# One load of a gate's attention outputs per head pair, sample transfers regrouped, and another emission order in a hybrid attention layer

## The chip, the cores and the metric

The kernel runs on one core of a Trainium2 chip. A core has four compute engines with queues of their own: TensorE (PE, matmuls and transposes into PSUM), VectorE (DVE), ScalarE (ACT) and GpSimd (POOL). A fifth queue, SyncE (SP), issues the transfers (DMA). Engines wait for each other through semaphores, and each queue runs in the order in which the program wrote it. The metric is the device time of one execution in microseconds, the median of several runs.

## The reference

One layer works on a prompt of 1024 tokens and on a sample of 32 tokens that has a cache of 512 past positions. The width is 1024, with 8 heads of 64 in group A (chunked band attention with a relative-position bias) and 8 in group B (stick-breaking attention). All is float32.

```python
hn = rmsnorm(h, g_pre)
qa, ka, va, ga, qb, kb, vb, gb = split(hn @ w_in)        # 1024 x 4096
oa = band_attention(qa, ka, va)       # softmax over the own 64-frame chunk and 8 before it
ob = stick_breaking(qb, kb, vb)       # w = sigmoid(z) * prod(sigmoid(-z)) over later keys
y  = concat(oa * silu(ga), ob * silu(gb)) @ w_out
h  = h + rmsnorm(y, g_post)
h  = h + sigmoid(h @ w_ple_gate) * (p @ w_ple)
```

The outputs are `h` of prompt and sample, and the new keys and values of both groups, for prompt and sample apart.

## The kernel before, in words

Every float32 product is made of three passes: an operand is split into a high part and the rest, and high x high, high x low and low x high are summed in PSUM. The names `wh`/`wl`, `hnh`/`hnl`, `wTh`/`wTl` and `kd`/`kl` are such pairs.

**Stages.** The first stage normalises nine row tiles of 128 (the ninth holds the 32 sample tokens), turns them into `hnh`/`hnl`, and makes the first columns of the input projection. Then come eight stages, one for each pair of heads (A0, B0, A1, B1, ... A3, B3). While stage n computes the attention of its pair (two heads), the projections q, k and v of the next pair (`col_steps`, matmuls named `mm_`, in three chunks of 352 tokens) fill TensorE. In stage 7 there is no next pair, and the eight gate projections (`mm_gA`, `mm_gB`) fill it. Two of the A stages and two of the B stages also carry the attention of the sample (`sample_attention`, four heads at a time). The last stage makes the second input (`ple`), the output projection (group products named `o0P` to `o3P`, seven products by a Strassen-like scheme for each half) and the gate projection (`g0P` to `g3P`), with normalisation and the final sum.

**Attention of a tile.** `scores` multiplies 128 queries with their keys into one or two PSUM banks of tag S (three buffers). Group B takes two sigmoids of each piece on ScalarE, a multiplying scan from the last key back on VectorE, and a product on GpSimd. Group A adds the bias on VectorE and takes an exponential on ScalarE. `weights_t` turns the weights: some tiles on TensorE (`ptw`), the others by a 32x32 transpose on VectorE, a store to a scratch tensor `swap`, and four reads back into `wTl`; ScalarE then casts to `wTh` and GpSimd or VectorE takes the rest into `wTl`. `values` multiplies with the values (`PV`) and stores the heads' outputs transposed in `o_dr`.

**Gates.** For each of three chunks of a gate, `mms` takes a tile `og` of two halves (tag `stg`, three buffers). One transfer loads the chunk's outputs from `o_dr`, and for group A two more load the reciprocal row sums `one_dr`, spread over 64 rows each. After the chunk's 24 matmuls ScalarE takes the sigmoid, VectorE multiplies it with the projection, GpSimd multiplies `og` with the sums and then both, and the result goes to `og_dr`. The last stage reads `og_dr` transposed.

**Sample.** New keys and values of the sample go to scratch tensors `ks_dr` and `vs_dr`, one for each pair. When the fourth pair of a group has stored its own, `sample_rows` writes all of them to the output in one transfer from scratch to output, in runs of 32 values. `sample_attention` loads its new values `vn` in two transfers, one for each of the two pairs that it covers.

**The order.** Nothing is emitted while the kernel is written down. A recorder collects all operations with their dependences. `order` plays them through a planner: each engine takes, among the operations that are ready by its cost table, the one with the least key. A key is a class (on TensorE attention goes before projections) and the operation's number in program order. `AHEAD_OF` adds an offset to that number, by engine and by the name of the tile that is written. Before, it has 73 rows with one value for each of ten stages (`STAGES`), 145 values of them other than zero. `moved` then shifts single operations in a queue by hand: `MOVES` has 34 entries (engine, place, distance), 21 of them on SP. The resulting queues are fixed: an operation whose input is late holds all that stands behind it on its engine.

Of the kernel before, what the change touches and what calls it, by code (L numbers as in the profile page):

```python
# [8 lines left out]
F32 = mybir.dt.float32  # L9
F32R = mybir.dt.float32r  # L10
AF = mybir.ActivationFunctionType
ALU = mybir.AluOpType

P = 128
# [13 lines left out]
STAGES = ("first", 0, 1, 2, 3, 4, 5, 6, 7, "last")  # L28
AHEAD_OF = {
    ("ACT", "Kh"): (0, 0, 0, 0, 430, 0, 0, 0, 200, 0),  # L30
    ("ACT", "L"): (0, 0, 46, 25, 452, 0, 112, 50, 0, 0),
    ("ACT", "Qfs"): (0, 0, 0, 0, 400, 0, 0, 0, 0, 0),
# [10 lines left out]
    ("ACT", "php"): (0, 0, 0, 0, 0, 0, 0, 0, 0, 175),  # L43
    ("ACT", "ple"): (0, 0, 0, 0, 0, 0, 0, 0, 0, 315),
    ("ACT", "stk"): (0, 0, 0, 0, 0, 96, -610, 0, 0, 0),
    ("ACT", "stq"): (0, 0, 0, 0, 0, -93, 0, 0, 0, 0),
    ("ACT", "stv"): (0, 0, -42, 0, 400, 0, 0, 0, 0, 0),
    ("ACT", "v"): (0, 0, 0, 0, 461, 0, 0, 0, 0, 0),
    ("ACT", "wTh"): (0, 93, 3, 89, 487, 0, 142, 52, -161, 0),
    ("ACT", "wh"): (0, 0, 405, 0, 0, 90, -480, -51, 364, 0),  # L50
    ("ACT", "whS"): (0, 0, 0, 0, 0, 0, 0, 0, 0, -93),
    ("ACT", "whs"): (0, 0, 0, 149, 0, 0, 0, 0, 0, 0),
    ("ACT", "x"): (0, 0, 0, 0, 0, 0, 0, 0, 0, -418),
    ("ACT", "xS"): (0, 0, 0, 0, 0, 0, 0, 0, 0, 25),
    ("DVE", "Kcs"): (0, 0, 0, 530, 0, 0, 0, 0, 100, 0),
    ("DVE", "Kl"): (0, 0, 0, 0, 0, 0, 0, 421, 0, 0),
    ("DVE", "L"): (0, 0, 0, 400, 0, 0, 0, 46, 0, 0),
    ("DVE", "Qls"): (0, 0, 0, 0, 0, 0, 0, 0, 54, 0),
# [3 lines left out]
    ("DVE", "diags"): (0, 0, 0, 400, 0, 0, 0, 0, 0, 0),  # L62
    ("DVE", "hnl"): (-100, 0, 0, 0, 0, 0, 0, 0, 0, 0),
# [4 lines left out]
    ("DVE", "sum"): (0, 0, 0, -109, 0, 0, 0, 0, 0, 0),  # L68
    ("DVE", "uu"): (0, 0, 0, 0, 0, 0, 0, 0, 0, -381),
    ("DVE", "vt"): (0, 165, 0, 0, -170, -75, 367, -88, 0, 0),  # L70
    ("DVE", "wTl"): (0, 0, 70, 0, 75, 50, 0, 100, -213, 0),
# [13 lines left out]
    ("POOL", "sgg"): (0, 0, 0, 0, 0, 0, 0, 0, 200, 0),  # L85
    ("POOL", "ug"): (0, 0, 0, 0, 0, 0, 0, 0, 0, -44),
    ("POOL", "wTl"): (0, 0, 0, 0, 400, 0, 465, 0, 0, 0),
# [38 lines left out]
def f(ap):  # L126
# [10 lines left out]
    ("ACT", 469, -1), ("ACT", 524, -1), ("SP", 513, 4), ("ACT", 365, 3), ("POOL", 302, 3),  # L137
    ("SP", 210, -2), ("SP", 325, 12), ("SP", 689, -5), ("POOL", 305, 5), ("SP", 598, 1),
    ("DVE", 228, -1), ("ACT", 822, 1), ("SP", 518, 4), ("SP", 532, 9),
# [223 lines left out]
class Recorder:  # L363
# [45 lines left out]
    def add(self, eng, what, args, kw):  # L409
# [29 lines left out]
        if writes:  # L439
            name = str(writes[0].buf.name)  # L440
            kind = (eng, name[:next((i for i, x in enumerate(name) if x.isdigit() or x in "AB_"), len(name))])
            o.kind = kind + (self.stage,)
            o.key = (o.key[0], o.key[1] + (AHEAD_OF[kind][STAGES.index(self.stage)] if kind in AHEAD_OF else 0), o.key[2])
# [185 lines left out]
def stream_step(  # L629
# [246 lines left out]

    def sample_rows(dst, squares):

        dma(dst[0, 0].rearrange("t h d -> t (h d)").rearrange("t (x f) -> x t f", f=32), squares.rearrange("p (g t) f -> (p g) t f", t=32))

    def keys_out(ab, p, src, o_p, o_s):
# [4 lines left out]
        def turn():  # L886
# [8 lines left out]
            if p == 3:  # L895
                sample_rows(o_s, ks_dr[ab])
# [36 lines left out]
    def col_steps(j):  # L933
# [7 lines left out]
        def mms(c, part):  # L941
# [9 lines left out]
            if k == "g" and part == 0:  # L951
                assert all(("V", pairs.index((ab, p)), h, g) in done for h in range(2) for g in range(len(SETS[ab])))
                if j in early:
# [5 lines left out]
                if ab == "A":  # L959
                    for h in range(2):  # L960
                        dma(og[h * HD:(h + 1) * HD, 1, 0:old], one_src(p, h, c * CH, old))
# [1167 lines left out]
```

## Time and profile before

| | us |
|---|---|
| median of 3 runs | 767.18 |
| lowest and highest run | 766.74, 767.9 |
| the profiled execution's own time | 766.89 |
| its span, first to last instruction | 765.1 |

The profile is of one execution, and the durations quoted below come from it. Its time is 0.29 us under the median; its span leaves out the 1.8 us around the first and the last instruction. The granted TensorE clock has a mean of 1.000 over the span. The page gives for each engine its busy time and its share of the span. A line of the page's groups has the operation, the tile that it writes and those that it reads, the shapes, the number of instructions, then busy time and mean ns of one, then the idle time of the engine just before them and what ended most of it. Nearly all instructions carry the one source line 623, at which the recorder emits them, so the groups are told apart by their tiles. Names of arenas stand for the tiles in them: `om` and `be` hold attention weights, and at the start also the input rows and their normalised form.

All transfers but instruction fetches go through the one queue of SP: 198322 packets and 164.44 MB, and by their packets' time they hold 73.8% of the sixteen DMA engines' span.

### The profile page before, as it was taken

What the parts mean: (1) busy time and instruction counts of PE and PEld (TensorE: products, weight loads), DVE (VectorE), ACT (ScalarE), POOL (GpSimd) and SP (SyncE); (2) the same over time, 40 slices, a digit from 0 to 9 for tenths busy, and PEclk for the clock granted to TensorE, in tenths of its full rate; (3) what the DMA queues carried; (4) which work ended last, traced back from release to release, by engine and by line L of the source; (5) the groups of instructions that cost most, each with busy time, mean ns of one, the idle gap of its engine ahead of it and who ended that gap; (6) DMA issues with size and microseconds to landing.
All of it is one profiled execution on the core that took longest, in us unless ns stands there. A gap on an engine that the chain in (4) does not pass through costs nothing.

```text
span 765.1 us, 14224 instructions
## 1 busy us (share of the span) xinstructions
PE 755.3 (99%) x4502; PEld 703.8 (92%) x4502; DVE 571.6 (75%) x1029; ACT 543.1 (71%) x1139; POOL 507.5 (66%) x547
## 2 busy tenths in 40 slices
PE   8999999999999999999999999999999999999997
PEld 6999999999999999999999998999998877888786
DVE  7727567687788778878797677778455787998975
ACT  6557877788688768898897677556438968766461
POOL 5734777995637657669994747788552549697533
PEclk9999999999999999999999999999999999999999
DMA  9737977759776557986859797879579967769644
GB/s 294 242 114 200 245 206 203 220 162 267 181 188 186 143 153 229 216 242 175 216 168 263 175 247 204 247 204 271 159 254 293 313 207 234 245 212 368 217 146 138
DMA packets 198397, 165.35 MB, mean 216 GB/s; under 512 B 65889, under 2 KB 165385, under 8 KB 198322
## 3 DMA queue, kind: packets, MB, share of 16 engines
q1 hardware_dynamic: 198322, 164.44, 73.8%
q8 instruction: 36, 0.59, 0.3%
q14 instruction: 39, 0.32, 0.1%
HBM read 105.72 MB, written 58.91 MB: 215 GB/s over the span
## 4 chain that ended last, share of the span: by engine, by line
PE 89%; DMA 4%; ACT 3%; POOL 2%; DVE 1%; SPq 0%; issue 0%; POOLq 0%; ACTq 0%; DVEq 0%
PE mm_kB L623 6%; PE mm_vA L623 6%; PE mm_gB L623 6%; PE mm_qB L623 6%; PE mm_gA L623 5%; PE mm_qA L623 5%; PE mm_kA L623 5%; PE PVB L623 4%; PE SA L623 4%; PE SB L623 3%; PE mm_vB L623 3%; PE PVA L623 3%; PE ple L623 3%; PE g1P L623 3%; PE o3P L623 3%; PE o1P L623 3%
## 5 line engine op out<-in xcount | busy, mean ns | idle before, releaser
L623 POOL TENSOR_TENSOR be<-be,om 128x1024 f32<-128x1024 f32 (+8 forms) x66 | 82.2, 1252 | 46.2 <-DVE om L623 14.2
L623 DVE TENSOR_TENSOR_SCAN om<-om,SB 128x384 f32<-128x384 f32 (+5 forms) x96 | 91.5, 964 | 19.7 <-ACT om L623 13.5
L623 POOL TENSOR_TENSOR wTl<-wTl,wTh 128x640 fp32r<-128x640 f32 (+2 forms) x42 | 72.5, 1744 | 13.8 <-ACT wTh L623 9.6
L623 ACT ACTIVATE om<-SB 128x384 f32<-128x384 f32 (+5 forms) x96 | 44.3, 494 | 12.8 <-DVE SB L623 7.9
L623 ACT ACTIVATE be<-SB 128x512 f32<-128x512 f32 (+5 forms) x96 | 45.5, 495 | 11.0 <-PE SB L623 7.4
L623 ACT ACTIVATE be<-be,statA 128x640 f32<-128x640 f32 (+3 forms) x64 | 44.4, 695 | 8.3 <-DVE statA L623 8.1
L623 DVE STREAM_TRANSPOSE om<-be 128x640 f32<-128x640 f32 (+2 forms) x48 | 42.9, 898 | 3.1 <-POOL be L623 1.9
L623 ACT CAST wTh<-wTl 128x640 fp32r<-128x640 f32 (+2 forms) x48 | 35.9, 778 | 8.7 <-DMA wTl<-swapA 7.0
L623 POOL TENSOR_TENSOR oB<-oB,oB 128x256 f32<-128x256 f32 x32 | 25.4, 817 | 15.2 <-DMA oB<-in_w_out_dram 15.2
L623 DVE CUSTOM_DVE_ANT_0 be<-SA,biasA 128x320 f32<-128x320 f32 (+3 forms) x64 | 30.1, 481 | 5.0 <-PE SA L623 3.9
L623 PE MATMUL SB<-kdB,LB 128*128 128x384 f32 (+5 forms) x96 | 32.4, 342 | 0.2 <-DVE om L623 0.2
L623 PE MATMUL SB<-kl,LB 128*128 128x384 f32 (+5 forms) x96 | 32.5, 345 | 0.0
L623 POOL TENSOR_TENSOR kl<-stkB,kdB 64x1024 fp32r<-64x1024 f32 x8 | 19.7, 2460 | 18.8 <-ACT kdB L623 18.7
L623 DVE TENSOR_TENSOR wTl<-ptwB,wTh 128x512 fp32r<-128x512 f32 (+3 forms) x48 | 26.0, 546 | 6.4 <-ACT wTh L623 5.7
L623 ACT CAST wTh<-ptwB 128x512 fp32r<-128x512 f32 (+3 forms) x48 | 22.9, 483 | 11.0 <-PE ptwB L623 10.4
L623 PE MATMUL SA<-kl,LA 128*128 128x320 f32 (+2 forms) x96 | 30.1, 316 | 0.0
L623 PE MATMUL SA<-kdA,LA 128*128 128x320 f32 (+2 forms) x96 | 29.9, 313 | 0.0
L623 DVE TENSOR_TENSOR SB<-SB,maskb 128x128 f32<-128x128 f32 x64 | 18.0, 293 | 15.2 <-PE SB L623 14.3
L623 DVE TENSOR_TENSOR wTl<-ptwA,wTh 128x512 fp32r<-128x512 f32 (+3 forms) x48 | 22.4, 478 | 8.7 <-ACT wTh L623 5.9
L623 PE MATMUL PVB<-wTl,v2B 128*128 128x256 f32 (+1 forms) x144 | 24.9, 295 | 0.0
L623 POOL TENSOR_TENSOR gB<-gB,gB 128x256 f32<-128x256 f32 x32 | 24.7, 794 | 0.1
L623 POOL TENSOR_TENSOR h<-h,x 128x512 f32<-128x512 f32 (+1 forms) x18 | 23.8, 1345 | 0.2 <-DVE h L623 0.2
(700 smaller groups left out, 2663.1 us busy)
## 6 DMA issues: line engine op xcount, KB each, us to landing
swapA<-om SPq DMA_DIRECT2D x8, 960.0 KB, 5.2
wTl<-swapA SPq DMA_DIRECT2D x32, 240.0 KB, 5.0
oB<-in_w_out_dram SPq DMA_DIRECT2D x16, 256.0 KB, 3.7
sum_dro<-oB SPq DMA_DIRECT2D x16, 256.0 KB, 3.6
gB<-in_w_ple_gate_dram SPq DMA_DIRECT2D x16, 256.0 KB, 4.0
sum_drg<-gB SPq DMA_DIRECT2D x16, 256.0 KB, 2.6
x<-in_x_prompt_dram SPq DMA_DIRECT2D x16, 256.0 KB, 3.7
h_dr<-h SPq DMA_DIRECT2D x8, 512.0 KB, 3.5
```

The source lines that it names most:

```text
L623: getattr(getattr(tc.nc, o.what[0]), o.what[1])(*args, **kw)
```

## The change

The gates load a pair's outputs once, as one tile of 1056 columns. The sums of group A have tiles of their own by chunk, of tag `bias` (two buffers). The `sample_rows` transfers are only noted down in the attention, and are issued in the last stage, one behind each of the first four products of the second output group. The two transfers of `vn` become one. The sigmoids of the second pass over the pieces run from the last piece to the first. The sigmoid of a part of the last tile goes to a PSUM bank of tag T (two buffers), and that of whole tiles stays in tag PV (one buffer). `AHEAD_OF` becomes 18 offsets by engine and name without stages, and `MOVES` keeps its first two entries. The matmuls, their number and their shapes are as before.

```diff
 AHEAD_OF = {
-    ("ACT", "Kh"): (0, 0, 0, 0, 430, 0, 0, 0, 200, 0),
-    ("ACT", "L"): (0, 0, 46, 25, 452, 0, 112, 50, 0, 0),
...
-    ("SP", "wr"): (34, 0, 0, 0, 0, 0, 0, -29, 0, 0),
+    ('ACT', 'o'): -25, ('ACT', 'oT'): 100, ('ACT', 'w'): -400, ('ACT', 'x'): -75,
+    ('DVE', 'newh'): 200, ('DVE', 'sq'): -400, ('POOL', 'bias'): -50, ('POOL', 'kl'): 100,
+    ('POOL', 'ksS'): -50, ('POOL', 'om'): -50, ('POOL', 'qsS'): 100, ('SP', 'be'): 25,
+    ('SP', 'biass'): 200, ('SP', 'kl'): 50, ('SP', 'ogg'): -400, ('SP', 'pp'): -400,
+    ('SP', 'stv'): -100, ('SP', 'vns'): -25,
 }
...
 MOVES = (
-    ("SP", 5, -1), ("ACT", 4, -1), ("SP", 465, 16), ("DVE", 499, -3), ("SP", 673, 6),
...
+    ("SP", 5, -1), ("ACT", 4, -1),
 )
...
-            o.key = (o.key[0], o.key[1] + (AHEAD_OF[kind][STAGES.index(self.stage)] if kind in AHEAD_OF else 0), o.key[2])
+            o.key = (o.key[0], o.key[1] + AHEAD_OF.get(o.kind, AHEAD_OF.get(kind, 0)), o.key[2])
...
+    behind = []
...
-                sample_rows(o_s, ks_dr[ab])
+                behind.append((o_s, ks_dr[ab]))
...
-                if j in early:
-                    og = box["og"] = at2.tile([P, 2, CH], F32, tag="bias", name=f"og{kind}{p}_{c}", bufs=2)
-                else:
-                    og = box["og"] = at2.tile([P, 2, CH], F32, tag="stg", name=f"og{kind}{p}_{c}", bufs=3)
+                if c == 0:
+                    box["og"] = at2.tile([P, T], F32, tag="stg", name=f"og{kind}{p}", bufs=3)
+                    dma(box["og"], o_dr[n])
                 old = min(CH, SEQ - c * CH)
-                dma(og[:, 0], o_dr[n][:, cs])
                 if ab == "A":
+                    box["one"] = at2.tile([P, CH], F32, tag="bias", name=f"one{kind}{p}_{c}", bufs=2)
                     for h in range(2):
-                        dma(og[h * HD:(h + 1) * HD, 1, 0:old], one_src(p, h, c * CH, old))
+                        dma(box["one"][h * HD:(h + 1) * HD, 0:old], one_src(p, h, c * CH, old))
...
-                og, old = box["og"], min(CH, SEQ - c * CH)
+                og, old = box["og"][:, cs], min(CH, SEQ - c * CH)
                 if ab == "A":
-                    nc.gpsimd.tensor_tensor(og[:, 0, 0:old], og[:, 0, 0:old], og[:, 1, 0:old], ALU.mult)
-                nc.gpsimd.tensor_tensor(sg, sg, og[:, 0], ALU.mult)
+                    nc.gpsimd.tensor_tensor(og[:, 0:old], og[:, 0:old], box["one"][:, 0:old], ALU.mult)
+                nc.gpsimd.tensor_tensor(sg, sg, og, ALU.mult)
...
-                sample_rows(o_s, vs_dr[ab])
+                behind.append((o_s, vs_dr[ab]))
...
-                for a, b, s in pieces:
+                for a, b, s in reversed(pieces):
                     nc.scalar.activation(w1[:, a:b], s, AF.Sigmoid)
...
-            for a in range(2):
-                dma(vn[:, a * P:(a + 1) * P].rearrange("t (g f) -> t g f", f=32), vs_dr[ab][2 * gi + a].rearrange("(g t) f -> t g f", t=32))
+            dma(vn.rearrange("t (g f) -> t g f", f=32), vs_dr[ab][2 * gi:2 * gi + 2].rearrange("a (g t) f -> t (a g) f", t=32))
...
-            sg = psum("PV", f"sg{self.t}")[0:n, part]
+            sg = psum("PV" if part == slice(0, 512) else "T", f"sg{self.t}")[0:n, part]
...
                 if m == 1 and pair == 1:
                     load_block("g", WHICH[prod])
+                if m == 1 and pair == 1 and behind:
+                    sample_rows(*behind.pop(0))
```

The scan over the weights, which stands right behind the sigmoids in both functions and is not changed, runs over the pieces in the reversed order before and after.

More of the change, by code (lines that the diff above doesn't have):

```diff
@@ L27 @@
 NT = 9
-STAGES = ("first", 0, 1, 2, 3, 4, 5, 6, 7, "last")
 AHEAD_OF = {
-    ("ACT", "Kh"): (0, 0, 0, 0, 430, 0, 0, 0, 200, 0),
-    ("ACT", "L"): (0, 0, 46, 25, 452, 0, 112, 50, 0, 0),
-    ("ACT", "Qfs"): (0, 0, 0, 0, 400, 0, 0, 0, 0, 0),
[10 rows of a table removed]
[L43 to L58, printed above, removed]
[3 rows of a table removed]
-    ("DVE", "diags"): (0, 0, 0, 400, 0, 0, 0, 0, 0, 0),
-    ("DVE", "hnl"): (-100, 0, 0, 0, 0, 0, 0, 0, 0, 0),
[4 rows of a table removed]
[L68 to L71, printed above, removed]
[13 rows of a table removed]
-    ("POOL", "sgg"): (0, 0, 0, 0, 0, 0, 0, 0, 200, 0),
-    ("POOL", "ug"): (0, 0, 0, 0, 0, 0, 0, 0, 0, -44),
-    ("POOL", "wTl"): (0, 0, 0, 0, 400, 0, 465, 0, 0, 0),
[15 rows of a table removed]
+    ('ACT', 'o'): -25, ('ACT', 'oT'): 100, ('ACT', 'w'): -400, ('ACT', 'x'): -75,
[3 more added lines that the diff above has]
+    ('SP', 'stv'): -100, ('SP', 'vns'): -25,
 }
@@ L132 @@
 MOVES = (
[4 rows of a table removed]
-    ("ACT", 469, -1), ("ACT", 524, -1), ("SP", 513, 4), ("ACT", 365, 3), ("POOL", 302, 3),
-    ("SP", 210, -2), ("SP", 325, 12), ("SP", 689, -5), ("POOL", 305, 5), ("SP", 598, 1),
-    ("DVE", 228, -1), ("ACT", 822, 1), ("SP", 518, 4), ("SP", 532, 9),
+    ("SP", 5, -1), ("ACT", 4, -1),
 )
@@ L1257, in scores @@
                     nc.scalar.activation(w0[:, a0:b0], s, AF.Sigmoid, scale=-1.0)
-                for a0, b0, s in pieces:
+                for a0, b0, s in reversed(pieces):
                     nc.scalar.activation(w1[:, a0:b0], s, AF.Sigmoid)
```

47 rows, old and new, of tables (AHEAD_OF, MOVES) are left out of this document.

## The prediction

> **What bounds the kernel now.** I read the page's busy table and chain first, then the waits of TensorE, then the stretches in which it was not full, and at last the rows around those places.
>
> ```profile
> span 765.1 us, 14224 instructions
> ...
> PE 755.3 (99%) x4502; PEld 703.8 (92%) x4502; DVE 571.6 (75%) x1029; ACT 543.1 (71%) x1139; POOL 507.5 (66%) x547
> ...
> PE   8999999999999999999999999999999999999997
> ...
> PE 89%; DMA 4%; ACT 3%; POOL 2%; DVE 1%; SPq 0%; issue 0%; POOLq 0%; ACTq 0%; DVEq 0%
> ```
>
> TensorE is busy for 755.3 of 765.1 us, so 9.8 us is all that it leaves. The next engine, VectorE, has 75%. The chain passes over SP's queue with 0%: issuing transfers does not set the end. The diff leaves every matmul as it is. So whatever the change saves must come out of these 9.8 us, while what it loses has no such limit. Of the page's 40 slices all but the first and the last read 9, at least 90%. Where the idle time lies, by stretches (bounds, length, then busy time and instructions of TensorE, weight loads, VectorE, ScalarE, GpSimd; granted clock, DMA share, GB/s):
>
> ```profile
> 0.00:20.00 20.00, 16.58 (x85) 13.62 (x86) 14.48 (x22) 12.77 (x24) 11.54 (x28) 1.00 0.91 298
> ...
> 440.00:460.00 20.00, 20.00 (x127) 19.51 (x126) 14.25 (x30) 15.44 (x33) 8.21 (x8) 1.00 0.97 246
> 460.00:480.00 20.00, 18.60 (x124) 17.96 (x123) 15.85 (x25) 15.96 (x38) 15.70 (x18) 1.00 0.81 211
> ...
> 760.00:765.10 5.10, 0.33 (x3) 0.12 (x1) 2.02 (x5) 0.76 (x2) 1.27 (x1) 1.00 0.36 129
> ```
>
> 3.4 us are idle at the start, 1.4 in one stall past 460, 4.8 behind the last matmul. The waits of TensorE (total, times, longest) name the same places:
>
> ```profile
> PE PVA L623 <- ACT wTh L623: 1.4, 1, 1.4
> PE idle L623 <- DVE newh L623: 1.3, 1, 1.3
> PE ptp L623 <- DMA pp<-in_p_prompt_dram: 1.1, 1, 1.1
> PE ple L623 <- ACT wph1True L623: 1.0, 1, 1.0
> PE SB L623 <- DVE om L623: 0.2, 1, 0.2
> ```
>
> Three of the five are of the start (1.3 + 1.1 + 1.0 = 3.4). In 440 us of attention TensorE waited visibly twice, 1.6 us together.
>
> **The change part by part. The end.** The last sum is cut in two pieces, and `Gate.out` puts the sigmoid of each in a bank. Before, it is tag PV with one buffer; now the pieces get tag T with two.
>
> ```profile
> 758.93 0.42 DVE L623 TENSOR_TENSOR uu<-uu,g3P 128x256 f32<-128x256 f32 x1 [0.76 <-PE g3P L623]
> ...
> 759.27 0.68 DVE L623 TENSOR_TENSOR uu<-sg,pl 128x512 f32<-128x512 f32 x1
> ...
> 759.98 0.39 ACT L623 ACTIVATE sg<-uu 128x256 f32<-128x256 f32 x1 [1.18 <-DVE uu L623]
> ...
> 760.37 0.42 DVE L623 TENSOR_TENSOR uu<-uu,g3P3b 128x256 f32<-128x256 f32 x1 [0.42 <-PE g3P3b L623]
> ...
> 761.16 0.39 ACT L623 ACTIVATE sg<-uu 128x256 f32<-128x256 f32 x1 [0.79 <-DVE uu L623]
> ...
> 762.04 0.42 DVE L623 TENSOR_TENSOR uu<-uu,hh 128x256 f32<-128x256 f32 x1
> ```
>
> The first piece's sum ends at 758.93 + 0.42 = 759.35, but its sigmoid starts at 759.98, when the product of the tile before (759.27 + 0.68 = 759.95) has left the one bank. With a bank of its own the sigmoid starts near 759.4, and that piece's product can follow at 759.95, before the last matmuls. The second sigmoid then starts right behind its sum, 760.37 + 0.42 = 760.8, instead of 761.16. With 0.39 for it and two steps of 0.42 VectorE ends at about 762.08 instead of 762.46: **-0.38 us**. Nothing at all, if VectorE's order leaves the first piece's addition ahead of the second's sum. I take -0.38.
>
> **The gates.** One load of a pair's whole row in place of three. The tile rows count what goes (durations are the queue's, min/median/max):
>
> ```profile
> L623 SPq DMA_DIRECT2D oggA<-one_dr x24: 444/464/604, 454.2 to 515.8; - x24
> L623 SPq DMA_DIRECT2D oggA<-o_dr x12: 326/516/1519, 453.8 to 514.7; - x12
> L623 SPq DMA_DIRECT2D oggB<-o_dr x12: 338/424/1336, 520.6 to 568.4; - x12
> ```
>
> 12 + 12 loads of outputs become 8; the 24 of the sums stay, now in a tile of their own. 16 issues less at 0.42 to 0.52 are some 7 to 8 us of SP's queue between 453 and 569, and the chain has 0% there: no gain by itself. What is late next: a pair's first chunk waits for three times the bytes.
>
> ```profile
> oggA<-o_dr SPq DMA_DIRECT2D x12, 176.0 KB, 3.6
> h_dr<-h SPq DMA_DIRECT2D x8, 512.0 KB, 3.5
> GP<-in_g_post_dram SPq DMA_DIRECT2D x1, 512.0 KB, 6.7
> ```
>
> 176 KB land in 3.6 us, 512 KB in 3.5 to 6.7, so 528 KB come up to 3.1 us later than a third does. Who waits is GpSimd's product, and behind it the store that the last stage reads. For the last pair this is covered by the work that TensorE has between the gates and the first output product (chain in order of time: start, length):
>
> ```profile
> 576.98 5.47 PE ple L623 x24
> ...
> 590.19 2.74 PE o0P L623 x12
> ```
>
> From 576.98 to 590.19 that is 13.2 us of cover against 3.1: **0**, and up to 3.1 without this cover. The sums' tiles of the A gates now turn in two buffers where three served: 12 chunks in 514.7 - 453.8 = 60.9 us are one each 5.5 us, so two buffers still give a load more than its 3.6. The price of the longer load for what stands behind it is a rival below.
>
> **Sample's values and rows.** Issue times again:
>
> ```profile
> L623 SPq DMA_DIRECT2D out_dram<-ks_drA x1: 1089/1089/1089, 371.7 to 371.7; - x1
> L623 SPq DMA_DIRECT2D vnsA<-vs_drA x4: 423/438/462, 201.2 to 429.7; - x4
> ```
>
> The new values come in one transfer for each of four sample steps: 4 issues of 0.44 go. The four stores of rows, up to 1.09 each, leave the attention and go to the first four products of the second output group in the last stage. They are moved past everything that SP holds between, the gates' loads and the first weights of the last stage included. There SP carries weights and rows of h, and up to 4.4 us of issuing would stand before them in four separate places; TensorE is full there and takes a product in 2.8 us (24 matmuls of two tiles in 5.5). At most 1.09 of one place could show if a weight slice came with no slack; I take **0**, since none of the page's slices there is below 9. Bounds: -0.5 to +1.1.
>
> **Sigmoid order.** The second pass over two pieces runs last piece first. Same instructions. The first piece's bank is let go one sigmoid later on ScalarE, but its scan is VectorE's last in any case:
>
> ```profile
> L623 DVE TENSOR_TENSOR_SCAN om<-om,SB 128x384 f32<-128x384 f32 (+5 forms) x96 | 91.5, 964 | 19.7 <-ACT om L623 13.5
> L623 ACT ACTIVATE be<-SB 128x512 f32<-128x512 f32 (+5 forms) x96 | 45.5, 495 | 11.0 <-PE SB L623 7.4
> ```
>
> A shift of 0.495 lies under a scan of 0.964: **0**.
>
> **The order anew.** All offsets by stage go, 18 plain ones come, and 32 of 34 moves go, on all five queues. Nothing in the trace shows this order, so I bound it. From below: all five waits gone, -5.0. From above, by the one handoff that was late:
>
> ```profile
> 450.43 2.62 SPq L623 DMA_DIRECT2D wTl<-swapA  x4
> ...
> 453.80 0.37 SPq L623 DMA_DIRECT2D oggA<-o_dr  x1
> ...
> 459.75 1.35 ACT L623 CAST wTh<-wTl 128x640 fp32r<-128x640 f32 x2 [3.48 <-DMA wTl<-swapA]
> ...
> 462.26 0.50 PE L623 MATMUL PVA<-wTh,v2A 128*128 128x512 f32 x1 [1.40 <-ACT wTh L623]
> ```
> ```profile
> L623 ACT CAST wTh<-wTl 128x640 fp32r<-128x640 f32 (+2 forms) x48 | 35.9, 778 | 8.7 <-DMA wTl<-swapA 7.0
> ```
>
> Weights turned through memory are issued at 450.43, cast at 459.75, and TensorE waits 1.40 us at 462.26. The gate's load is issued behind them at 453.80, so the stall isn't the gates' and their edit doesn't lift it. 48 such tiles are cast in a run, and one in 48 was late. Were it four more, +5.6. Between -5.0 and +5.6 I take the value of the nearest row, one late handoff as now: **0**.
>
> **Sum**: -0.38 against the profiled execution, whose time was 766.89 (1.8 around its span): 766.5. It lay 0.29 under the median 767.18 of the runs shown, so the median should be **766.8**, by 0.05% less.
>
> **A page against the trace.** At the start the offset of +200 for the cleared tile `newh` sets its memset behind two others:
>
> ```profile
> 0.87 0.38 DVE L623 MEMSET newh<- 128x384 f32 x1 [0.87 <-PEq L2117]
> ...
> 1.30 2.93 PE L623 MATMUL idle<-newh 128*128 128x256 f32 x12 [1.30 <-DVE newh L623]
> 1.41 0.91 DVE L623 MEMSET wTl<- 128x1024 f32 x1 [0.16 <-issue]
> ```
>
> Two memsets of 0.91 and their gaps put the 12 idle matmuls about 2 us later; TensorE's later waits of 1.1 and 1.0 take that up, to 0.1. The granted clock reads 1.00 in every stretch, but an idle matmul takes 2.93 / 12 = 0.244 us from start to start. The Trainium skill (TensorE: Matmul & The Clock Gate, "Part 1: The HAM clock gate") says the array starts at half rate and needs about 3.4 us of activity. By that rule a later warm-up is paid again in slow first matmuls; an estimate from it is under 2 us, and the sum by it would be above mine by that much. The profile's 1.00 cannot confirm it.
>
> **The rivals.** (A) *The new order also lifts the waits of the attention*: 1.4 + 0.2 go with the 0.38, 765.2. For it: the cast at 459.75 waited 3.48 for transfers alone, which an earlier issue cures. Against: 0.97 of the DMA engines' time was taken there. (B) *The start gets shorter*: `sq` 400 places ahead on VectorE brings the normalised rows sooner, and 1.1 + 1.0 go with the 0.38: 764.7. Against: the first wait there is for a load, not for VectorE. (C) *The longer load stands in front* (slower): SP's offset -400 puts 528 KB ahead of the next transposed weights, 352 KB more than now. At the 246 GB/s of 440 to 460 that is 1.47 us for each handoff whose slack is smaller. And the load waits until every output of its pair is stored; behind it on SP stand the reads of turned weights and the next gates' weights, for which casts and then TensorE wait. By the loads' rows four A gates begin within 61 us, so up to six of eight run beside the last pair's attention. It decides from the first uncovered one on; two give 2.9 - 0.38, 769.7. The Trainium skill (DMA: Bandwidth & Descriptors, "Queues, rings and completion order") says that each DMA engine consumes one queue's descriptors in ring order; this is the mechanism of that rule, and no row here shows a small transfer pass a large one. (D) *The order without its placings lets handoffs slip* (slower): three more of the 48 turned tiles come late, 3 x 1.40 - 0.38: 771.0. It decides from the first on; for it speaks that each queue runs in a fixed order, so that TensorE, 99% full, cannot win back what one late cast costs. Against: ScalarE and VectorE have a quarter of their time free. (E) *The change doesn't do what it says*: the whole-row load still needs every output of its pair stored, and the sums come by chunks as before, so the gates start no sooner; then the time is the forecast's.
>
> **How the numbers follow.** Forecast (with E) 0.28, A 0.23, B 0.12, C 0.11, D 0.26. A measurement of this kernel tells about 0.2% from no change, 1.5 us: 765.65 to 768.7 is the same. Faster is A + B = 0.35, same 0.28, slower C + D = 0.37. The range runs from 763.0 (B with the waits of A) to 772.4 (four late handoffs and 0.38 won). About 0.04 are left out below, where all five waits would go, and 0.14 above. The forecast's own range is 765.7 to 768.6.
>
> **What would show it.** Right: TensorE busy about 755 again, the same five waits or others of their size, the two last sigmoids 0.6 and 0.35 sooner against the last matmul, loads of 528 KB eight times, the four stores in the second output group. Wrong: new TensorE waits on `wTh` or `wTl` of a us each (D), or on such casts right behind a 528 KB load (C); idle time of the first stretch under 2 us (B). Matmuls that grow slower would break the whole argument.

## The result, and the profile after

The changed kernel takes **802.86 us** (median of 4 runs, 799.04 to 804.9), the kernel before 767.12 us beside it (766.74 to 767.9): a ratio of 1.0451, 95% interval 1.0424 to 1.0478. It is 36 us slower. The prediction was 766.8 us, with a range to 772.4. The profiled run took 804.9 us, 1.8 around its span, and is the slowest of the four.

The page of the changed kernel: the span, the busy times, the 40 slices of TensorE and of its granted clock, and the chain by engine.

```profile
span 803.1 us, 14211 instructions
...
PE 772.8 (96%) x4502; PEld 711.9 (89%) x4502; DVE 572.8 (71%) x1029; ACT 543.7 (68%) x1139; POOL 505.9 (63%) x547
...
PE   8999999999989998989999997999999999999997
...
PEclk9999999999999998999999999999999999999999
...
PE 75%; DMA 9%; DVE 4%; ACT 4%; POOL 3%; SPq 3%; issue 2%; DVEq 0%; ACTq 0%; POOLq 0%
```

VectorE, ScalarE and GpSimd are busy for as long as before, to 2 us: no work was added. TensorE is idle for 803.1 - 772.8 = 30.3 us where it was for 9.8, and its 4502 matmuls take 772.8 us where they took 755.3. So of the 38.0 us of the span 20.5 are idle time and 17.5 are the same matmuls taking longer. The chain has given 14 of TensorE's hundredths to transfers, queues and the other engines.

TensorE's waits of the changed kernel (total, times, longest):

```profile
PE PVA L548 <- ACT wTh L548: 6.4, 5, 2.2
PE SB L548 <- DVE om L548: 3.5, 2, 2.9
PE idle L548 <- DVE newh L548: 3.5, 1, 3.5
PE SA L548 <- DVE statA L548: 2.7, 4, 1.2
PE mm_gA L548 <- ACT stvB L548: 2.0, 2, 1.4
```

There were five waits of 5.0 us; now there are 23 of 24.8. Turned weights (`wTh`, `wTl`) lead, as rival D said, but with all their groups they are 8.1 of the 24.8 us, a third: scans (`om`), maxima (`statA`) and copies out of banks (`stvB`) are late as well. The start of the last matmul of each projection, from the trace, tells where the time goes (kA is the projection of the keys of group A, gA that of its gate):

| us | before | after | later by |
|---|---|---|---|
| kA of pair 0 | 55.24 | 56.42 | 1.2 |
| vB of pair 1 | 226.24 | 232.94 | 6.7 |
| kA of pair 2 | 246.56 | 259.82 | 13.3 |
| kB of pair 2 | 300.99 | 330.85 | 29.9 |
| vB of pair 2 | 347.55 | 370.76 | 23.2 |
| gA of pair 0 | 474.00 | 507.64 | 33.6 |
| gB of pair 3 | 576.65 | 611.58 | 34.9 |
| the last matmul | 760.05 | 797.82 | 37.8 |

TensorE's queue has another order now, so a row is not idle time alone: kB of pair 2 is 29.9 us later and vB of the same pair 23.2, because other matmuls stand ahead of the first. The loss falls in the attention, in jumps. The gates, which the change rewrote, lose 1.3 us between their first and last projection, the last stage 2.8. The jump at 490 us lies within the first gate's projection, but its longest wait, 2.18 us, is for turned weights of the last pair's attention. The stretches of 10 us around the jumps (columns as before; the granted clock is the third number from the end):

```profile
200.00:210.00 10.00, 8.27 (x47) 7.92 (x46) 6.71 (x14) 4.23 (x10) 5.47 (x4) 0.86 0.98 186
...
220.00:230.00 10.00, 10.00 (x66) 9.54 (x65) 6.44 (x23) 9.13 (x23) 3.66 (x5) 1.00 0.83 248
230.00:240.00 10.00, 6.19 (x33) 5.35 (x32) 6.39 (x8) 9.28 (x17) 5.00 (x6) 0.89 0.56 106
240.00:250.00 10.00, 10.00 (x54) 9.89 (x53) 7.38 (x12) 5.81 (x17) 7.68 (x11) 0.76 0.39 132
...
310.00:320.00 10.00, 6.92 (x26) 4.03 (x26) 9.75 (x27) 9.90 (x20) 4.61 (x3) 0.82 0.36 103
320.00:330.00 10.00, 10.00 (x62) 9.90 (x60) 7.32 (x21) 7.81 (x22) 1.94 (x4) 0.84 0.66 191
...
490.00:500.00 10.00, 7.60 (x37) 7.20 (x38) 7.25 (x10) 7.93 (x18) 9.37 (x7) 0.83 0.65 184
```

Two things stand in these rows. TensorE is idle for 1.7 to 3.8 us in each jump. And in and behind it the clock reads 0.76 to 0.89, where it was 1.00 throughout before: in 240 to 250 TensorE is busy for all of the 10 us and gets 54 matmuls done, where 220 to 230 has 66. Over the whole span the mean granted clock is 0.986 against 1.000, some 803.1 x 0.014 = 11 us of clock. About one of these lies behind the last matmul (the clock is 0.52 from 801 to 803 us), so the clock accounts for some 10 of the 17.5 us; what makes the matmuls longer by the other 7 or 8 is not shown.

One jump in full, that at 230 us. TensorE's queue in the changed kernel (start, length):

```profile
233.10 0.60 PE L548 MATMUL ptwA<-ident,be 128*128 128x128 f32 x4
236.59 0.50 PE L548 MATMUL SB<-kdB,LB 128*128 128x512 f32 x1 [2.89 <-DVE om L548]
...
238.59 2.61 PE L548 MATMUL PVA<-wTh,v2A 128*128 128x512 f32 x8 [0.92 <-ACT wTh L548]
...
241.53 2.55 PE L548 MATMUL mm_kA<-hnh,wh_kA 128*128 128x352 f32 x8
```

The same place of the kernel before:

```profile
228.57 0.60 PE L623 MATMUL ptwA<-ident,be 128*128 128x128 f32 x4
228.93 0.73 PE L623 MATMUL mm_kA<-hnh,wh_kA 128*128 128x352 f32 x3
...
232.08 1.46 PE L623 MATMUL mm_kA<-hnh,wh_kA 128*128 128x352 f32 x8
233.37 1.39 PE L623 MATMUL PVA<-wTh,v2A 128*128 128x512 f32 x8
```

The first and longer wait, 2.89 us, is that of a score product (`SB`) for VectorE's scan (`om`); the second, 0.92, is for the turned weights, which are still on their way behind the last transposes (`ptwA`). The kernel before fills that time with 27 matmuls of the next projection, 228.93 to 233.37, and PVA follows without a gap. In the changed kernel these stand behind PVA. What would have held them at an earlier place too is to be seen in ScalarE's queue:

```profile
236.56 1.98 ACT L548 CAST wTh<-wTl 128x640 fp32r<-128x640 f32 x3 [0.67 <-DMA wTl<-swapA]
238.44 0.59 ACT L548 ACTIVATE om<-SB 128x512 f32<-128x512 f32 x1
...
239.41 0.45 ACT L548 COPY stvB<-mm_vB 128x352 f32<-128x352 f32 x1
```

The copy of `mm_vB` at 239.41 frees the bank that the projection's first matmul needs. The matmuls that it waits for had ended by 229.4, but ScalarE is busy for 9.28 of the 10 us from 230, and the copy stands behind that work, in which casts waited 0.67 us for a transfer. In the kernel before both such copies came ahead of those casts, at 224.33 and 227.58 against 230.37:

```profile
224.33 0.54 ACT L623 COPY stvB<-mm_vB 128x352 f32<-128x352 f32 x1
...
227.58 0.46 ACT L623 COPY stvB<-mm_vB 128x352 f32<-128x352 f32 x1
...
230.37 1.98 ACT L623 CAST wTh<-wTl 128x640 fp32r<-128x640 f32 x3
```

### The profile page after: what moved, and what is told of

Read it like the earlier page. It is cut to its first block, busy times and chain, and to the rows that moved or that the text cites. A ratio compares the mean times of both kernels' runs of the same rounds, so it can differ in the third digit from the quotient of the medians.

```text
span 803.1 us, 14211 instructions
## 1 busy us (share of the span) xinstructions
PE 772.8 (96%) x4502; PEld 711.9 (89%) x4502; DVE 572.8 (71%) x1029; ACT 543.7 (68%) x1139; POOL 505.9 (63%) x547
## 4 chain that ended last, share of the span: by engine, by line
PE 75%; DMA 9%; DVE 4%; ACT 4%; POOL 3%; SPq 3%; issue 2%; DVEq 0%; ACTq 0%; POOLq 0%
PE mm_gB L548 6%; PE mm_kA L548 5%; PE mm_gA L548 5%; PE mm_qA L548 4%; PE mm_vA L548 4%; PE mm_qB L548 4%; PE mm_vB L548 4%; PE PVA L548 4%; DMA wTl<-swapA 3%; PE PVB L548 3%; PE mm_kB L548 3%; PE SB L548 3%; SPq L548 3%; PE g1P L548 2%; PE o3P L548 2%; PE o1P L548 2%
## 5 line engine op out<-in xcount | busy, mean ns | idle before, releaser
L548 POOL TENSOR_TENSOR wTl<-wTl,wTh 128x640 fp32r<-128x640 f32 (+2 forms) x42 | 71.7, 1722 | 23.2 <-ACT wTh L548 19.7
L548 ACT ACTIVATE om<-SB 128x384 f32<-128x384 f32 (+5 forms) x96 | 46.3, 496 | 19.6 <-DVE SB L548 15.6
L548 ACT ACTIVATE be<-be,statA 128x640 f32<-128x640 f32 (+2 forms) x64 | 44.4, 696 | 15.1 <-DVE statA L548 14.8
L548 ACT ACTIVATE be<-SB 128x384 f32<-128x384 f32 (+5 forms) x96 | 46.3, 498 | 5.2 <-PE SB L548 3.8
L548 PE MATMUL SA<-kdA,LA 128*128 128x320 f32 (+2 forms) x96 | 32.1, 338 | 3.0 <-DVE statA L548 2.7
L548 DVE CUSTOM_DVE_ANT_0 be<-SA,biasA 128x320 f32<-128x320 f32 (+2 forms) x64 | 29.7, 476 | 3.7 <-PE SA L548 2.9
L548 ACT COPY otB<-PVB 64x256 f32<-64x256 f32 x32 | 11.0, 367 | 24.4 <-PE PVB L548 24.1
L548 PEld LDWEIGHTS PVA<-wTh,v2A 128*128 128x128 f32 x96 | 16.8, 200 | 9.4 <-ACT wTh L548 8.2
```

Source lines behind the costliest of these rows:

```text
L548: getattr(getattr(tc.nc, o.what[0]), o.what[1])(*args, **kw)
```

## The experiments

**Theory 1**: the loss is the order of the queues alone. **Theory 2**: it is the edits, above all the gates' long loads (rival C) and the moved rows. Inside theory 1 it was asked what an order is (1a) and how a late handoff becomes so dear (1b).

### The edits without the order, the order without the edits

`edits_alone` has every line of the change but the reversed sigmoid pass, and its queues are a list that holds the operations of each engine in the order of the kernel before. The whole-row loads stand where the first chunk's load stood.

```diff
-        for e, i, d in MOVES:
-            seq[e].insert(i + d, seq[e].pop(i))
+        place, named = 0, {n: o for n, o in enumerate(self.ops)}
+        for e, n in zip(("PE", "ACT", "DVE", "POOL", "SP"), COUNTS):
+            seq[e] = [named[x] for x in QUEUES[place:place + n]]
+            place += n
```

> All edits of the gates, the sample's values and rows and the last bank, but every engine's queue in the order of the kernel before (the order is written out as a list; the reversed second sigmoid pass is left out of it). Theory 1, the loss is all in the order: 766 to 767.5 us, TensorE's waits about 5 us, the tail 0.2 to 0.4 us shorter. Theory 2, the longer gate load or the moved rows cost (rival C): over 769 us, new TensorE waits between 480 and 570 us on weights behind a 528 KB load; had the edits the whole loss, about 803 us.

Measured: 774.02 us against 766.35, ratio 1.0100 (1.0082 to 1.0117). That is neither theory's number. 28 of the 36 us are gone, 7.7 stay. Between the last projection of the attention and that of the gates the profile keeps its distance from the kernel before to 0.6 us, so the 7.7 are not the gates'. TensorE runs the same 4502 matmuls in the same sequence in both, so each new delay can be put at one matmul, the three largest +0.9 at 114, +1.5 at 256 and +1.3 at 345 us of the kernel before. The first, followed back, ends at a copy on ScalarE. The kernel before, and then this one:

```profile
100.02 0.64 ACT L623 COPY otA<-PVA 64x256 f32<-64x256 f32 x2
```
```profile
100.73 0.37 ACT L723 COPY otA<-PVA 64x256 f32<-64x256 f32 x1
...
102.04 0.37 ACT L723 COPY otA<-PVA 64x256 f32<-64x256 f32 x1 [0.94 <-DVE otA L723]
```

The two copies ran back to back before; now the second waits 0.94 us for VectorE's sum, which reads the same bank of PVA. The order inside each queue is the same. What differs is the order in which the operations of ScalarE and VectorE are written against each other, since `moved` still merged the queues by the planner's ranks. Three copies into `otA` (2.7 us in all) and two into `otB` wait for VectorE here, where none waited visibly before. So `edits_in_place` lists all operations in one sequence, that of the kernel before:

```diff
-        rank = {id(o): n for n, o in enumerate(out)}
-        seq = {e: [o for o in out if o.eng == e] for e in ("PE", "ACT", "DVE", "POOL", "SP")}
-        turn = {e: [rank[id(o)] for o in seq[e]] for e in seq}
-        for e, i, d in MOVES:
-            seq[e].insert(i + d, seq[e].pop(i))
+        named = {n: o for n, o in enumerate(self.ops)}
+        given = [named[n] for n in GIVEN]
+        rank = {id(o): n - len(out) for n, o in enumerate(out)}
+        rank.update((id(o), n) for n, o in enumerate(given))
+        seq = {e: [o for o in given if o.eng == e] for e in ("PE", "ACT", "DVE", "POOL", "SP")}
+        turn = {e: [rank[id(o)] for o in seq[e]] for e in seq}
```

> The same edits as in edits_alone, and not only each engine's queue but also the order in which the operations of different engines are written against each other is that of the kernel before. (In edits_alone that second order was left to the planner, and there ScalarE's second copy of PVA at 101 us waited 0.94 us for VectorE's sum on the same bank, which in the kernel before it did not.) Theory 1a, the 7.7 us of edits_alone are waits between engines that share a bank: 766 to 767.5 us, its stalls at 114, 256 and 345 us gone. Theory 2, the edits themselves cost them: 773 to 775 us again.

Measured: 767.44 us against 767.65, ratio 0.9998 (0.9980 to 1.0016). These waits for VectorE and the delays at 114, 256 and 345 us are gone, and TensorE's waits are these four:

```profile
PE idle L721 <- DVE newh L721: 1.3, 1, 1.3
PE ptp L721 <- DMA pp<-in_p_prompt_dram: 0.9, 1, 0.9
PE ple L721 <- ACT wph1True L721: 0.9, 1, 0.9
PE PVA L721 <- ACT wTh L721: 0.7, 1, 0.7
```

In the order of the kernel before, the edits cost and bring nothing that can be measured (the interval is 0.2% to each side). Theory 2 falls, and 1a stands: the order across engines alone makes the 1.0% between these two kernels.

The other half, the order without the edits: the operations of the kernel before with the 18 plain offsets and two moves.

```diff
-    ("ACT", "Kh"): (0, 0, 0, 0, 430, 0, 0, 0, 200, 0),
...
+    ('ACT', 'o'): -25, ('ACT', 'oT'): 100, ('ACT', 'w'): -400, ('ACT', 'x'): -75,
...
-    ("SP", 5, -1), ("ACT", 4, -1), ("SP", 465, 16), ("DVE", 499, -3), ("SP", 673, 6),
...
+    ("SP", 5, -1), ("ACT", 4, -1),
```

> The operations of the kernel before, with the 18 plain offsets and the two moves of the change. Theory 1, the order: 795 to 810 us, TensorE's waits 20 to 30 us, on turned weights above all. Theory 2, the edits: 766 to 769 us.

Measured: 806.47 us, ratio 1.053 (1.048 to 1.058), with 28 waits of 28.1 us and a clock of 0.989. The order alone loses at least as much as the whole change, 40 us. Turned weights were expected above all; with 6.1 us for the first product they lead again, and are again no more than a part.

### What carried the order

Three kernels split it: the table by stage kept and only the 32 moves gone (`moves_gone`), no offset at all (`no_offsets`, with `AHEAD_OF = {}`), and the changed operations under the old table (`table_kept`).

> The kernel before with its whole table of offsets by stage, but with only the first two of its 34 moves. Within theory 1: if the table carries the order, 767 to 771 us; if the 32 hand moves carry it, near 800 us. Theory 2 (edits) has 767 us.

Measured: 773.11 us, ratio 1.0079 (1.0053 to 1.0104). The 32 moves are worth 6.8 us, a little more than was expected.

> The operations of the kernel before with no offset at all and the two moves. If the 18 plain offsets are a poor start for these operations, this is as fast as order_alone or faster, 795 to 807 us; if they are worth something, it is slower than 807 us. Either way far from 767 us, when the table by stage carries the order.

Measured: 804.48 us, ratio 1.0480 (1.0454 to 1.0506). The 18 plain offsets are worth nothing on these operations (806.47 with them), and the table by stage some 31 us.

> The changed kernel with the table of offsets by stage of the kernel before in place of its own 18 offsets, and the two moves. If the table alone is what was lost, 767 to 771 us. If a table found for one list of operations does not fit another list, 785 us or more, with waits of TensorE in other places than in the changed kernel.

Measured: 802.93 us, ratio 1.0477 (1.0455 to 1.0498), as slow as the changed kernel, with its longest wait in another place:

```profile
453.59 2.61 PE L617 MATMUL PVA<-wTh,v2A 128*128 128x512 f32 x8 [5.92 <-ACT wTh L617]
```

The table that gives 773.11 us on the operations before gives 802.93 on the changed ones, which have 20 transfers fewer on SP's queue (16 loads of the gates, 4 of the sample's values) and the reversed sigmoid pass. So it holds for the list of operations that it was found for. Why it does not fit the other one was not separated: the offsets are added to the number that an operation has in the program, and the change shifts these numbers, but it also changes what is ready when.

### How a late handoff becomes so dear

`filler_behind` is the kernel before, with one thing changed in its sequence of TensorE (matmuls in the order of the queue):

```diff
-    mm_kA x27, PVA x10
+    PVA x10, mm_kA x27
```

> The kernel before with one thing changed: the first ten matmuls of PVA on the turned weights, which start at 233.4 us, stand ahead of the 27 projection matmuls that run from 228.9 us in place of behind them. Theory 1b: TensorE waits 4 to 4.5 us at one place and never wins it back, and the granted clock falls below 0.95 in the 10 us behind it: 771 to 774 us. Rival, TensorE takes the time back from its other waits: under 769 us.

Measured: 773.35 us (769.1 to 775.87, 10 runs), ratio 1.0062 (1.0041 to 1.0083), where the other theory had under 769. The profiled run, in stretches of 4 us:

```profile
228.00:232.00 4.00, 0.55 (x5) 0.31 (x4) 3.96 (x6) 3.69 (x7) 1.42 (x1) 0.89 0.66 229
232.00:236.00 4.00, 4.00 (x15) 3.81 (x16) 1.60 (x2) 1.28 (x3) 4.00 (x4) 0.50 0.61 172
236.00:240.00 4.00, 4.00 (x21) 4.00 (x20) 0.00 (x0) 0.47 (x2) 2.42 (x4) 0.76 0.01 4
240.00:244.00 4.00, 4.00 (x26) 3.91 (x25) 2.02 (x4) 2.26 (x7) 0.00 (x0) 1.00 0.01 2
```

TensorE stands from 228.4 to 231.8 us. Then it works at a clock of 0.50 and 0.76 for 8 us: 15 and 21 matmuls where the same view of the kernel before has 27 and 30. At the end of this projection it is 5.68 us behind the kernel before, having been 0.81 ahead of it, so in this execution, the slowest of the ten, the single exchange costs 6.5 us: some 3.5 of waiting and 3.0 of clock. By the medians it is 5.7, and the fastest of the ten runs, 769.1 us, has a mean clock of 0.999. Up to the next stall, over 200 us, not a tenth is won back (5.65 at the end of the last projection).

`filler_part` puts 18 of the 27 behind PVA and leaves 9 ahead.

> As filler_behind, but only 18 of the 27 projection matmuls stand behind the ten matmuls of PVA, so the stall is some 2 us where it was 3.7 there. If the granted clock falls only behind long stalls, it stays at 1.00 in the 10 us behind this one and the projection that is cut in two ends 2 us later, 769 us. If 2 us are enough, as behind the stall at 204 us of the changed kernel, the clock reads 0.7 to 0.9 in one 4 us stretch and the projection ends about 3 us later, 770 us.

Measured: 771.57 us, ratio 1.0056 (1.0035 to 1.0078). In the profiled run, of 768.63 us, the stall is 2.0 us and the clock reads 1.00 behind it:

```profile
228.00:232.00 4.00, 2.02 (x13) 1.68 (x12) 3.96 (x6) 3.71 (x8) 1.60 (x2) 1.00 0.67 242
232.00:236.00 4.00, 4.00 (x28) 3.95 (x27) 1.44 (x2) 1.96 (x6) 4.00 (x3) 1.00 0.56 156
```

From the projection before to the end of this one 2.3 us are lost (0.98 ahead, then 1.28 behind). The other four runs of this kernel have a mean clock of 0.996 to 0.998 and 770.37 to 772.57 us, so the profiled one, at 1.000, is the cheapest of the five. Their lower means suggest that behind a stall of 2 us the clock falls in some executions and not in others; no trace shows where it fell in them. Neither of the two expectations holds for all runs.

The other way round, `filler_ahead` is the changed kernel with four copies of ScalarE and groups of projection matmuls put ahead of the work that held them, at five stalls:

```diff
-    ACT: ... om<-SB, be<-SB, wTh<-wTl x3, om<-SB, be<-SB, stvB<-mm_vB
+    ACT: stvB<-mm_vB, ... om<-SB, be<-SB, wTh<-wTl x3, om<-SB, be<-SB
-    PE: SB x4, PVA x10, mm_kA x13
+    PE: mm_kA x18, SB x4, PVA x10
...
```

> The changed kernel in its own order, but at five stalls (204, 234, 314, 355 and 490 us) 4 to 21 projection matmuls that stood behind the waiting matmul are put ahead of it, with four copies out of banks of the projections put ahead of the work that held them on ScalarE. Theory 1b, a late handoff costs because ready matmuls and the copies that free their banks are queued behind it: the fill takes about 11 us of idle time and some of the lowered clock behind it, 785 to 795 us. Rival, the chain through ScalarE, VectorE and the store is what is slow and TensorE only waits for it: over 799 us, the waits come back later.

Measured: 796.66 us, ratio 1.0366 (1.0338 to 1.0394) against 1.0451 of the changed kernel: 0.85% less, 6.5 us. That is between the two expectations, 1.7 us past the upper end of the first. In the profile, of the fastest of its four runs against the slowest of the changed kernel's, the span is 10.4 us shorter (792.7) and the mean clock 0.996 in place of 0.986, so most of what was won is clock (0.010 x 793 = 8 us). But TensorE still waits 20.6 us:

```profile
PE ptwA L721 <- DVE wTl L721: 3.9, 3, 1.8
PE SB L721 <- DVE om L721: 3.6, 4, 1.8
...
PE PVA L721 <- POOL wTl L721: 2.5, 2, 1.3
PE PVA L721 <- ACT wTh L721: 1.5, 1, 1.5
```

The named waits went, and their neighbours came: both theories hold a part. Fill that is held behind a late handoff explains a fifth of the loss by this run; in the rest of it the chain through VectorE, ScalarE and GpSimd is itself later than TensorE needs it, and other fill has to be found there.

Last, two small ones. `start_first` puts the memset of `newh` first on VectorE again, in the changed kernel's own order.

> The changed kernel in its own order with the memset of newh first on VectorE, as before, instead of third. If the start costs what the trace shows, the idle matmuls start 2.1 us sooner and the first projection ends 0.8 to 1.2 us sooner; the whole time falls by no more than that, 801 to 803 us, or by nothing if the later stalls take it.

Measured: one run of 802.65 us, no difference to be told from the changed kernel's 799.04 to 804.9. In its trace the idle matmuls start 2.15 us sooner, and the first projection ends 0.45 us sooner, less than was expected; the last matmul is 2.2 us sooner, within the spread of the runs. `best` is `edits_in_place` with ten more matmuls of the first gate ahead of the PVA that waits at 460 us.

> The edits in the order of the kernel before (edits_in_place), with ten more projection matmuls of the first gate ahead of the ten of PVA that wait at 460 us. The wait of 0.7 to 1.4 us there goes: 766 to 767 us, 0.1 to 0.2% under the kernel before, at the bound of what can be told from no change. If something else is as late there, 767.5 us.

Measured: 767.63 us (12 runs) against 766.62, ratio 1.0006 (0.9993 to 1.0019): no gain. The stall at 460 is gone, and a wait of 1.0 us for GpSimd's part of the same weights stands a few matmuls on:

```profile
460.00:464.00 4.00, 4.00 (x28) 3.98 (x27) 1.66 (x3) 2.73 (x5) 1.92 (x2) 1.00 0.79 216
464.00:468.00 4.00, 2.98 (x19) 2.60 (x18) 3.51 (x4) 1.83 (x5) 4.00 (x4) 1.00 0.83 252
```

A wait of 1.2 us at 430 us, which neither `edits_in_place` nor the kernel before has in its profile, lies ahead of the moved matmuls, so the exchange did not make it.

No version was found that beats the kernel before.

**What stays open.** Which engine's queue carries most of the loss wasn't tried: the queues wait for one another in both directions, and one of them in the changed order does not run with four in the old. The reversed sigmoid pass was measured only inside the changed kernel. And of the 36 us `filler_ahead` gives back 6.5; the rest is told apart from that by this one run's waits alone, and no run takes it away piece by piece.

## Why the prediction was wrong, point by point

**The failing step is the order anew.** The prediction wrote "Between -5.0 and +5.6 I take the value of the nearest row, one late handoff as now: **0**". The order is worth the whole 36 us: `order_alone` has the loss without the edits, `edits_in_place` the edits without the loss. The bound of +5.6 was four late handoffs at 1.40 each, from the one that the kernel before still had. That row shows what an order costs where it is good, and it can't bound one that is not there yet. Three things were missed:

- The size of one. A handoff without its cover costs 5.7 us by the medians of `filler_behind` and 6.5 in its profile, not 1.40. The row for it was in the trace of before, as work: the 27 matmuls from 228.93 to 233.37 that stand between the last transpose and PVA are 4.4 us of cover, and PVA came 1.0 us behind its last cast (230.37 + 1.98). The A heads have 8 such rounds in four pairs; without cover for any, 8 x 4.4 = 35 us would have been a bound from above, as an estimate from that one row. That it comes near the measured 36 is luck: two thirds of the changed kernel's waits are not for turned weights, and the clock is not in it.
- The clock. The sum has no term for it, since "the granted clock reads 1.00 in every stretch"; that held for the full queue of the kernel before. Some 10 us are lost to it in the changed kernel.
- That the order across engines is a part of the order. It alone made the 7.7 us of `edits_alone`.

**Rival D** named the right side and the right mechanism, "so that TensorE, 99% full, cannot win back what one late cast costs", and this is what `filler_behind` shows over 200 us. Its size, three times 1.40 = 4.2 us, was too small by a factor of more than eight. "Against: ScalarE and VectorE have a quarter of their time free" carried no weight: they have it still (68% and 71%), and are late at the places that count.

**Rivals A and B** fall: the changed order lifts no wait, and the start is 1.2 us longer at the end of the first projection, where "to 0.1" was said of what would remain of the later idle matmuls. Of these, `start_first` gives back 0.45. The lower end of the range, B with the waits of A, comes to 764.7 - 1.6 = 763.1 by its own terms, not 763.0.

**Rival C** falls. The eight loads of 528 KB are there, and they land later than the 3.6 us of a third, as was worked out:

```profile
oggA<-o_dr SPq DMA_DIRECT2D x4, 528.0 KB, 6.8
oggB<-o_dr SPq DMA_DIRECT2D x4, 528.0 KB, 5.8
```

But `edits_in_place` has them too, and loses nothing. The Trainium skill's rule of ring order that was weighed there (DMA: Bandwidth & Descriptors, "Queues, rings and completion order") is neither confirmed nor contradicted: no run here shows a loss by it.

**The gates, the sample's values and rows** were put at 0, and `edits_in_place` agrees to 0.2%. One detail was wrong: the four stores of rows do not leave in the last stage. The diff records them there, but the planner fills SP's queue by what is ready, and in the trace of after they are issued between 399.6 and 514.6 us. In `edits_in_place` they are issued between 372.8 and 486.6 and cost nothing that can be measured; the changed kernel's places were not tried alone.

**The end** was put at -0.38 us. The sigmoid of the first piece does start 0.6 us sooner against the last matmul, as worked out, but VectorE ends 0.08 sooner, not 0.38. The changed kernel:

```profile
797.82 0.29 PE L548 MATMUL g3P3b<-gB,wlS4g 128*128 128x256 f32 x1
...
798.48 0.88 DVE L548 TENSOR_TENSOR uu<-uu,hh 128x256 f32<-128x256 f32 x1
...
799.28 0.41 DVE L548 TENSOR_TENSOR uu<-sg,pl 128x256 f32<-128x256 f32 x1
799.73 0.42 DVE L548 TENSOR_TENSOR uu<-uu,hh 128x256 f32<-128x256 f32 x1
```

From the last matmul's start to the end of the last addition it is 800.15 - 797.82 = 2.33 us, against 762.46 - 760.05 = 2.41 before. The first piece's addition takes 0.88 in place of 0.42 and stands between the second sigmoid and its product. "Nothing at all, if VectorE's order leaves the first piece's addition ahead" had the cause, but the wrong operation: it is the product that waits, not the sum.

**What would show it** held. "New TensorE waits on `wTh` or `wTl` of a us each (D)" came, and "matmuls that grow slower would break the whole argument" came as well, through the clock.

## What to carry to other kernels

Where one engine is 99% busy and every queue has a fixed order, the order is itself a tuned part: price its loss by the cover that it provides at each handoff (the work between the last step that feeds a relay and the first that needs it), not by the few waits that it has left. Offsets and moves that are tied to the numbers of operations were found for one list of operations and can stop fitting when a small edit changes it, as in `table_kept`, so the finished sequence should be kept, and new operations placed into it by hand, as `edits_in_place` does. And when an order is held fixed for a comparison, the order across engines has to be held as well as that inside each queue.

## What the runs showed of the hardware

**A stall can cost twice: the wait, and a lower clock behind it.** In stretches of 1 us the granted clock of the changed kernel reads 1.00 or 0.50, and something between only where it changes; 0.68 or 0.86 in a longer stretch is a mean. It is 0.50 from 207.2 to 210.6, 237.9 to 244.7, 316.4 to 323.2 and 493.9 to 497.3 us, which is 3.4 or 6.8 us each time, and each of the jumps has one of these. In `filler_behind` it is 0.50 for 6.8 us behind the wait of 3.45.

The length of a wait does not tell whether the clock falls. It fell behind one of 1.73 us at 204 us of the changed kernel, behind one of 1.83 at 466 us of `filler_behind` (0.75 and 0.82 in the next 8 us), and at 316 us of the changed kernel among short waits, of which the longest was 1.16. It stayed at 1.00 behind the 1.40 of the kernel before, the 1.98 of `filler_part`, and a wait of 2.68 us in `moves_gone`, which is the idle time in the first of these rows:

```profile
320.00:330.00 10.00, 7.32 (x47) 6.84 (x47) 5.08 (x16) 5.67 (x10) 4.46 (x5) 1.00 1.12 312
330.00:340.00 10.00, 10.00 (x65) 9.52 (x65) 7.26 (x12) 9.82 (x24) 6.60 (x8) 1.00 0.54 106
```

Around the end of the longest wait, 5.92 us in `table_kept`, it read 0.50 (452 to 456 us). The ten runs of `filler_behind`, one and the same program, lie between 769.1 us at a mean clock of 0.999 and 775.87 us at 0.993. What decides between two waits of like length is not shown. The Trainium skill (TensorE: Matmul & The Clock Gate, "Part 1: The HAM clock gate") says that the clock halves after an idle window of about 3.4 us, and that the window runs freely. The reading of 0.50 and its lengths of 3.4 and 6.8 us agree with it, and so does the spread between runs; that single waits of less than 2 us were enough does not.
